# RWKV-7's triangular block inverses: transposed blocks, inversion by columns, scaling after the blocks are gathered

## The chip, the cores and the metric

The kernel runs on one core of a Trainium2 chip. The metric is the device time of one execution in microseconds (us). The kernel before was timed in 3 runs: 1908.01, 1912.06 and 1916.1 us, median 1912.06. One further execution was taken with the hardware profiler; all views quoted below come from it.

A core has five engines that each work through their own instructions in order: TensorE (PE; its weight loads are shown as PEld), VectorE (DVE), ScalarE (ACT), GpSimd (POOL) and SyncE (SP), which here issues DMA transfers. They wait for each other by semaphores.

## The reference

A small model of two layers is run in float32 over a prompt and a sample batch: a gated-delta-net mixer, a ConvFFN, an RWKV-7 mixer, a ConvFFN. The change touches only the RWKV-7 mixer, whose recurrence per head is

```python
def rwkv_step(S, xs):                       # S: [value, key]
    r, d, k, v, kk, a = xs
    sa = einsum('bhvk,bhk->bhv', S, -kk)
    S  = S * d[..., None, :] + sa[..., None] * (kk * a)[..., None, :] \
         + v[..., None] * k[..., None, :]
    return S, einsum('bhvk,bhk->bhv', S, r)
```

where `kk` is a key scaled to unit norm: it is divided by the root of its sum of squares. The kernel does not step through time. It takes chunks of 64 tokens. Inside a chunk the removal terms `sa` of the 64 tokens depend on each other through a strictly triangular 64x64 matrix L of key-by-key products, each row scaled by the inverse of the key's squared norm, and the kernel needs the inverse of I + L for each of 16 heads and each of 9 chunks (chunk 0 has 48 tokens: three blocks of 16).

## The kernel before, in words

The activations stand as 560 columns (prompt and samples) on 128 partitions. Dense layers split every float32 weight tile into a high part (`hi`, line 70, ACT) and a low part (`lo`, line 71, DVE), and multiply with three reduced-precision float32 passes on PE (`dense_g`, line 115, tile `pd`): for every weight tile two columns' halves, four matmuls with `hi` and two with `lo`.

The RWKV mixer lies between about 975 and 1440 us of the profiled span. Its dense work is written as "slots", and the chunk work as "chains", Python generators that a small scheduler (`Weave`, line 359) interleaves: a step says how much PE time it takes and how long its result needs, and a step that isn't due leaves room for the next dense piece. So the order on PE is fixed when the kernel is built; a tile framework then puts the instructions of every engine in an order by a simulated timeline. On the chip each engine simply takes them in that order and waits where an operand isn't ready.

The stages that matter here, for each half G of the heads (G=0 and G=1, 8 heads each):

- `early(G)` (from line 1379): for each of the 9 chunks, eight key-by-key products per chunk on PE (line 1392), masked by DVE out of PSUM into a tile `L` of a ring of two (line 1396), each head's rows scaled by the inverse squared norms `ssq` on ACT (line 1398: 8 instructions for each chunk, 144 in all), and the diagonal blocks sent by DMA to DRAM (`LI0`, line 1373, for chunk 0; `LI`, line 1378). Each chunk has two 32x32 blocks per head.
- `inverse0(G)` gathers the 24 blocks of 16x16, one block on each partition, into the tile X (line 1422), inverts them, and stores them to `UI0` (line 1425). `inverse(G)` does the same with 128 blocks of 32x32 (lines 1406 and 1409). Both halves use the same tile X, so that its loads wait for the stores before. The results are scattered to the matrices A (line 1415, called XX in the trace for one pair of chunks, and line 1430), whose 64x64 form is then made by `merge` (line 1435) for two chunks at a time, four times in a chain: a DVE transposition (line 1439), 16 matmuls (line 1443), an ACT copy (1444), 16 matmuls (line 1448), an ACT copy (line 1449).
- `tri_inplace` (line 1011) is the inversion: GpSimd sets the diagonal to 1 (line 1014); then, row by row from the last one up, a DVE multiplication (line 1023) makes the products for the sums in a tile `tmp` (called `tri` in the trace) and a DVE reduction along the free axis (line 1025) puts the negated sums into X. The multiplication reads X along rows and writes `tmp` transposed (`t.rearrange("p n j -> p j n")`), so that the reduction can run along contiguous elements: the distance between two elements written one after the other is the length of a sum. The tile `tmp` holds 384 elements for each partition, so that a row of 32x32 blocks is done in up to three pieces.
- `rec(G)` (from line 1571) is the recurrence over the chunks. Its DVE steps (lines 1565, 1644, 1652 among them) alternate with PE steps (lines 1624, 1633, 1642, 1651), and it needs the merged blocks. While `rec(0)` does its first chunks, DVE is still inverting the blocks of `inverse(1)`.

Of the kernel before, what the change touches and what calls it, by code (L numbers as in the profile page):

```python
# [8 lines left out]
F32 = mybir.dt.float32  # L9
F32R = mybir.dt.float32r  # L10
I32 = mybir.dt.int32
AF = mybir.ActivationFunctionType
ALU = mybir.AluOpType
AX = mybir.AxisListType
# [3 lines left out]
P = 128  # L18
AHEAD, WB = 1, 2
NRAW = 4  # L20
T = 560
# [988 lines left out]

def tri_inplace(E, X, tmp, n, R):

    nc = E.nc
    nc.gpsimd.memset(X.rearrange("p a b -> p (a b)")[:n, 0:R * R:R + 1], 1.0)  # L1014
    N = tmp.shape[1]
    for i in range(R - 2, -1, -1):
        m = R - 1 - i
        step = min(m, N // m)
        for c1 in range(R, i + 1, -step):
            c0 = max(c1 - step, i + 1)  # L1020
            m1, k = c1 - i - 1, c1 - c0
            t = tmp[:n, :m1 * k].rearrange("p (a b) -> p a b", a=k)
            nc.vector.tensor_tensor(t.rearrange("p n j -> p j n"), X[:n, i + 1:c1, c0:c1],  # L1023
                                    X[:n, i, i + 1:c1].unsqueeze(2).to_broadcast([n, m1, k]), op=ALU.mult)
            nc.vector.tensor_reduce(X[:n, i, c0:c1], t, axis=AX.X, op=ALU.add, negate=True)
        yield


# [22 lines left out]
def rwkv(E, xp, norm, x_dram, sink):  # L1051


    nc, I, O = E.nc, E.I, E.O
    st = ExitStack()
    with st:
        ar = E.pool("rw", 1, stack=st)
        dp = E.pool("rwd", 1, DRAM, stack=st)
        pg = E.pool("pr", 4, PSUM, stack=st)
        bank = bank_of(pg)  # L1060

        KR = ar.tile([P, KD, 9, 2, 64], F32, tag="KR", name="KR")
# [43 lines left out]
        pa = dense(E, [KD], xs, 280)  # L1106
# [48 lines left out]
        for i, r in enumerate((dn, up)):  # L1155
            nc.scalar.activation(th[i][r], la[r], AF.Copy if i == 0 else AF.Tanh)
            if i:
                nc.scalar.activation(la[r], la[r], AF.Tanh)
            nc.vector.tensor_tensor(tl[r], la[r], th[i][r].bitcast(F32), op=ALU.subtract)
            nc.scalar.activation(th[i][(up, dn)[i]], la[r], AF.Copy)  # L1160


        XX, H = big(E, F32, "XX", 0), big(E, F32, "H", 1)
# [129 lines left out]
        def sums(m, sq):  # L1293

            pt = bank([9, 2])
            for c in range(9):
                o, n = col64(c)
                nc.tensor.matmul(pt[64:128, c, :], lhsT=sq[:, o:o + 64], rhs=blk2, start=True, stop=True)
            nc.vector.tensor_copy(ssq[64:128, :, 2 * m:2 * m + 2], pt[64:128])
            if m % 4 == 3:  # L1300
                hs = slice(2 * m - 6, 2 * m + 2)
                q = ssq[64:128, :, hs]
                nc.vector.tensor_scalar(q, q, 1e-6, None, op0=ALU.add)
                nc.vector.reciprocal(q, q)
                nc.vector.tensor_scalar(nw[64:128, :, hs], q, -1.0, None, op0=ALU.mult)
                W.chain(early(m // 4))
            yield 0.6, 0.5, 1


        stA = ExitStack()  # L1310
# [71 lines left out]
        def early(G):  # L1382

            while not decayed >= set(range(4 * G, 4 * G + 4)):
                yield None
            for c in range(9):
                n = col64(c)[1]
                pa = [bank([4, 64]) for hh in range(2)]
                for u in range(4):
                    for hh in range(2):  # L1390
                        r = slice(64 * hh, 64 * hh + 64)
                        nc.tensor.matmul(pa[hh][up, u, :n], lhsT=KB[r, 4 * G + u, c, 1, :], rhs=KR[r, 4 * G + u, c, 1, :n], start=True, stop=True)
                L = E.xp.tile([P, T], F32, tag="s", name="L", bufs=2)[up, :512].rearrange("p (h t) -> p h t", h=8)[:, :, :n]
                mk = mask0[up, 1] if c == 0 else mask[up, 64:128]
                for hh in range(2):
                    nc.vector.tensor_tensor(L[:, hh::2], pa[hh][up, :, :n], mk.unsqueeze(1).to_broadcast([64, 4, n]), op=ALU.mult)
                for h in range(8):
                    nc.scalar.activation(L[:, h], L[:, h], AF.Copy, scale=ssq[up, c, 8 * G + h:8 * G + h + 1])
                to_inverse(G, c, L)
                yield 0.9, E.d2, 2  # L1400

# [2 lines left out]
        def inverse(G):  # L1404
            X, tmp = B["X"], B["tmp"]
            nc.sync.dma_start(out=X, in_=LI[G].rearrange("j c h i t -> (j c h) i t"))
            for _ in tri_inplace(E, X, tmp, P, 32):
                yield 0, E.d3, 0
            nc.sync.dma_start(out=UI[G].rearrange("j c h i t -> (j c h) i t"), in_=X)
# [10 lines left out]
        def inverse0(G):  # L1420
            X = B["X"].rearrange("p a b -> p (a b)")[:24, :256].rearrange("p (a b) -> p a b", a=16)
            nc.sync.dma_start(out=X, in_=LI0[G].rearrange("j h i t -> (j h) i t"))
            for _ in tri_inplace(E, X, B["tmp"], 24, 16):
                pass
            nc.sync.dma_start(out=UI0[G].rearrange("j h i t -> (j h) i t"), in_=X)
# [437 lines left out]
def prep(a):  # L1863
# [56 lines left out]
    def rput(name, m):  # L1920
        rc[:, RC[name]:RC[name] + m.shape[1]] = m
    rput("mask", np.concatenate([i64[:, None] <= a64[None], i64[:, None] < a64[None]], 1) * 1.0)
    b64 = np.where(i64 < 48, np.minimum(i64 // 4, 8), 9)
    same = b64[:, None] == blk[None]
    rput("mask0", np.concatenate([same & (i64[:, None] <= a48[None]), same & (i64[:, None] < a48[None])], 1) * 1.0)
    b = (ar[:, None] // 64 == ar[None] // 64) * 1.0
    rput("blk", b)
# [112 lines left out]
```

## Time and profile before

| | before |
|---|---|
| median of 3 runs | 1912.06 us |
| the profiled execution | 1913.3 us |
| its span on the core | 1911.3 us |
| mean granted TensorE clock | 0.95 |
| PE busy | 1801.1 us (94%) |
| DVE busy | 1154.5 us (60%) |
| ACT busy | 803.9 us (42%) |
| GpSimd busy | 369.0 us (19%) |

A line `L1023` names line 1023 of the kernel before. A group such as `tri<-X` names the tile written and the tile read. `x124` is a count. In a view by windows each engine has its busy time in a stretch of the span and its instructions; `PEclk` is the clock that TensorE was granted, 1.00 being full speed. In a timeline the brackets at the end of a row hold the idle time of that engine just before it and what ended it. In the chain that ended last, each row is a piece of work or a transfer on which the end of the program depended.

The four inversions lie at 1008.4 to 1040 us (`inverse0(0)`), 1047.1 to 1131.4 us (`inverse(0)`), 1138.7 to 1156.5 us (`inverse0(1)`) and 1162.8 to 1231.5 us (`inverse(1)`).

### The profile page before, as it was taken

The numbers are of one execution on the slowest core, as the hardware profiler recorded it, in microseconds if no ns is written. First come the engines' busy times: TensorE is split into PE (matmuls) and PEld (weight loads), VectorE is DVE, ScalarE is ACT, GpSimd is POOL, SyncE is SP. The second block draws the span as 40 slices with busy tenths as digits, with TensorE's granted clock in tenths as the row PEclk, the third lists the DMA queues.
The fourth block names the chain that finished last, engine by engine and source line by source line (L and its number), as shares of the span: only waits on it lengthen the run. The fifth ranks groups of instructions, "written<-read, shape, count | busy, mean of one in ns | idle before, by whom it ended". The sixth has DMA issues, their size and how long they took to land.

```text
span 1911.3 us, 36670 instructions
## 1 busy us (share of the span) xinstructions
PE 1801.1 (94%) x14673; PEld 1718.5 (90%) x14673; DVE 1154.5 (60%) x2221; ACT 803.9 (42%) x1779; POOL 369.0 (19%) x616
## 2 busy tenths in 40 slices
PE   7999999999999999998989999799997999999996
PEld 6889998789999999998778997788786999999996
DVE  6698973875555553337787977874555555554223
ACT  4766434442222222222976535554644322222221
POOL 3442403621222220013110000021001111111011
PEclk9999998999999999999898999896898999999998
DMA  4233232433222223444122244332235322223331
GB/s 131 76 91 93 70 90 104 150 122 120 82 89 89 80 87 104 120 155 98 48 70 62 70 117 121 98 91 80 78 102 163 123 89 89 89 88 91 99 109 67
DMA packets 128010, 186.13 MB, mean 97 GB/s; under 512 B 63088, under 2 KB 75376, under 8 KB 127840
## 3 DMA queue, kind: packets, MB, share of 16 engines
q10 hardware_dynamic: 34448, 111.63, 18.7%
q1 hardware_dynamic: 93392, 72.17, 13.0%
q8 instruction: 116, 1.90, 0.4%
q14 instruction: 54, 0.44, 0.1%
HBM read 151.56 MB, written 32.18 MB: 96 GB/s over the span
## 4 chain that ended last, share of the span: by engine, by line
PE 76%; DVE 12%; ACT 3%; DMA 3%; issue 1%; POOL 0%; SPq 0%; DVEq 0%; ACTq 0%
PE pd L115 56%; PE pd L138 3%; PE pg L1353 1%; DVE lo L71 1%; PE pg L1739 1%; PE pg L1628 1%; DVE it L425 1%; PE pg L1624 1%; PE pg L1651 1%; PE pg L1642 1%; DVE tri L1023 1%; PE pg L835 1%; PE pg L1633 1%; DVE cv L593 1%; DMA xd<-xo 1%
## 5 line engine op out<-in xcount | busy, mean ns | idle before, releaser
L115 PE MATMUL pd<-x,hi 128*128 128x280 f32 (+7 forms) x4768 | 837.5, 297 | 23.5 <-ACT hi L70 9.1
L115 PEld LDWEIGHTS pd<-x,hi 128*128 128x128 f32 (+1 forms) x4768 | 695.4, 192 | 30.8 <-ACT hi L70 9.3
L115 PE MATMUL pd<-x,lo 128*128 128x296 f32 (+5 forms) x2384 | 516.4, 297 | 5.6 <-DVE lo L71 5.6
L70 ACT ACTIVATE hi<-raw 128x1024 fp32r<-128x1024 f32 (+3 forms) x218 | 219.8, 1009 | 481.7 <-PE pd L115 447.4
L115 PEld LDWEIGHTS pd<-x,lo 128*128 128x128 f32 (+1 forms) x2384 | 382.9, 192 | 9.9 <-DVE lo L71 6.8
L71 DVE TENSOR_TENSOR lo<-raw,hi 128x1024 fp32r<-128x1024 f32 (+3 forms) x218 | 255.7, 1173 | 219.1 <-ACT hi L70 212.6
L218 POOL TENSOR_TENSOR s<-s,sq 128x560 f32<-128x560 f32 (+2 forms) x30 | 50.8, 1693 | 303.7 <-ACT sq L216 273.9
L304 DVE TENSOR_TENSOR gp<-pd,s 128x528 f32<-128x528 f32 (+1 forms) x44 | 30.8, 701 | 105.9 <-PE pd L115 105.9
L115 PE MATMUL pd<-hl,hi 128*128 128x280 f32 (+1 forms) x448 | 93.5, 290 | 0.0
L115 PE MATMUL pd<-hh,hi 128*128 128x280 f32 (+1 forms) x448 | 93.3, 290 | 0.0
L115 PE MATMUL pd<-hh,lo 128*128 128x280 f32 (+1 forms) x448 | 93.3, 290 | 0.0
L316 ACT ACTIVATE gs<-cv 128x528 f32<-128x528 f32 (+1 forms) x44 | 28.1, 639 | 147.3 <-DVE cv L314 147.3
L115 PE MATMUL pd<-hb,hi 128*128 128x280 f32 (+1 forms) x512 | 85.8, 290 | 0.0
L115 PEld LDWEIGHTS pd<-hb,hi 128*128 128x128 f32 x512 | 72.8, 188 | 0.0
L115 PEld LDWEIGHTS pd<-hh,lo 128*128 128x128 f32 x448 | 70.8, 188 | 0.0
L115 PEld LDWEIGHTS pd<-hh,hi 128*128 128x128 f32 x448 | 70.6, 188 | 0.0
L115 PEld LDWEIGHTS pd<-hl,hi 128*128 128x128 f32 x448 | 70.5, 188 | 0.0
L319 POOL TENSOR_TENSOR gs<-gs,s 128x560 f32<-128x560 f32 (+1 forms) x44 | 60.8, 1382 | 38.1 <-ACT gs L317 38.1
L322 DVE TENSOR_TENSOR h<-pd,gs 128x560 f32<-128x560 f32 (+1 forms) x44 | 32.1, 730 | 57.0 <-POOL gs L319 57.0
L308 POOL COPY fnew<-gp 128x2 f32<-128x2 f32 x44 | 8.1, 185 | 291.5 <-DVE gp L304 291.5
L1023 DVE TENSOR_TENSOR tri<-X 128x4 f32<-128x4 f32 (+26 forms) x124 | 56.0, 451 | 5.2 <-POOL X L1014 2.2
L138 PE MATMUL pd<-os,hi 128*128 128x280 f32 x256 | 52.8, 303 | 2.5 <-ACT os L183 1.9
(539 smaller groups left out, 3039.6 us busy)
## 6 DMA issues: line engine op xcount, KB each, us to landing
raw<-w_up ACTq DMA_DIRECT2D x88, 512.0 KB, 3.3
raw<-w_in ACTq DMA_DIRECT2D x32, 512.0 KB, 3.3
raw<-w_down ACTq DMA_DIRECT2D x32, 512.0 KB, 3.6
raw<-w_down ACTq DMA_DIRECT2D x16, 384.0 KB, 3.0
kbd<-kst SPq DMA_DIRECT2D x18, 256.0 KB, 2.0
KB<-kbd SPq DMA_DIRECT2D x18, 256.0 KB, 3.0
xd<-xo SPq DMA_DIRECT2D x16, 280.0 KB, 2.1
raw<-gdn_out ACTq DMA_DIRECT2D x8, 512.0 KB, 3.3
```

Of the source, the lines that this page charges most:

```text
L70: nc.scalar.activation(hi[:R, :kt, :M], raw[:R, :kt, :M], AF.Copy)
L71: lo_eng.tensor_tensor(lo[:R, :kt, :M], raw[:R, :kt, :M], hi[:R, :kt, :M].bitcast(F32), op=ALU.subtract)
L115: nc.tensor.matmul(ps[b][:M, :c1 - c0] if isinstance(ps, list) else ps[:M, b, :c1 - c0], lhsT=w[:, kk, :M], rhs=x[:, c0:c1], start=(k == 0 ...
L138: nc.tensor.matmul(ps[:, b, :c1 - c0], lhsT=a, rhs=x[:, c0:c1], start=(k == i == 0), stop=(k == len(xs) - 1 and i == 2))
L218: nc.gpsimd.tensor_tensor(self.acc[:, :self.w], self.acc[:, :self.w], sq, op=ALU.add)
L304: nc.vector.tensor_tensor(two(gp[:, m0:]), pm, two(s[:, mo:mo + ml]), op=ALU.mult)
L316: nc.scalar.activation(gs[:, mo:mo + ml], cv[:, m0 - 2:], AF.Silu)
L319: nc.gpsimd.tensor_tensor(gs, gs, s[:, :n_main], op=ALU.mult)
L322: nc.vector.tensor_tensor(two(h), ps[:, :, :hw], two(gs), op=ALU.mult)
L425: nc.vector.tensor_tensor(t.rearrange("p n j -> p j n"), U[:n, i:R, c0:], L[:n, i, i:R].unsqueeze(2).to_broadcast([n, m, k]), op=ALU.mult)
L593: nc.vector.scalar_tensor_tensor(cv, gp[:, i:i + 584], cw[i], cv, op0=ALU.mult, op1=ALU.add)
L1023: nc.vector.tensor_tensor(t.rearrange("p n j -> p j n"), X[:n, i + 1:c1, c0:c1], X[:n, i, i + 1:c1].unsqueeze(2).to_broadcast([n, m1, k]), ...
```

## The change

Five things are done differently.

1. In `early`, the two operands of the key-by-key matmuls change places, so that the blocks come out transposed (and on partitions 0 to 63). The mask is a transposed constant `maskT`, loaded once. The 144 ACT scalings are gone.
2. The inverse squared norms are brought into the order of the blocks: `by_block`, once for each half, copies `ssq` on ACT, transposes it on PE (72x64), copies it on ACT and stores it to DRAM (`Dd`).
3. `inverse` and `inverse0` load them with two and three small DMAs for each half, and one DVE multiplication for each scales all of X (128x1024 and 24x256).
4. `tri_inplace` goes by columns from the first to the last: the products are now written as they are read, contiguously, and the reduction puts a column of sums into X, whose elements lie one row of X apart.
5. As the sums of a column take the place of the upper half, a DVE memset sets the row's lower half to zero after each column.

By the sizes in the code, the 32x32 inverse has 43 multiplications and 43 reductions over 8671 elements for each partition in place of 47 and 47 over 8450, and 31 memsets; the 16x16 inverse has 15 and 15 over 1240 elements as before, and 15 memsets. Over the four inversions that is 116 multiplications in place of 124, 116 reductions in place of 124, 19822 elements in place of 19380, and 92 memsets.

```diff
 def tri_inplace(E, X, tmp, n, R):
     nc.gpsimd.memset(X.rearrange("p a b -> p (a b)")[:n, 0:R * R:R + 1], 1.0)
     N = tmp.shape[1]
-    for i in range(R - 2, -1, -1):
-        m = R - 1 - i
-        step = min(m, N // m)
-        for c1 in range(R, i + 1, -step):
-            c0 = max(c1 - step, i + 1)
-            m1, k = c1 - i - 1, c1 - c0
-            t = tmp[:n, :m1 * k].rearrange("p (a b) -> p a b", a=k)
-            nc.vector.tensor_tensor(t.rearrange("p n j -> p j n"), X[:n, i + 1:c1, c0:c1],
-                                    X[:n, i, i + 1:c1].unsqueeze(2).to_broadcast([n, m1, k]), op=ALU.mult)
-            nc.vector.tensor_reduce(X[:n, i, c0:c1], t, axis=AX.X, op=ALU.add, negate=True)
+    for j in range(1, R):
+        i = 0
+        while i < j:
+            w = j - i
+            k = min(w, N // w)
+            t = tmp[:n, :k * w].rearrange("p (a b) -> p a b", a=k)
+            nc.vector.tensor_tensor(t, X[:n, i:i + k, i:j], X[:n, j, i:j].unsqueeze(1).to_broadcast([n, k, w]), op=ALU.mult)
+            nc.vector.tensor_reduce(X[:n, i:i + k, j], t, axis=AX.X, op=ALU.add, negate=True)
+            i += k
+        nc.vector.memset(X[:n, j, 0:j], 0.0)
         yield
...
+        maskT = nw[dn].rearrange("p a b -> p (a b)")[:, :112]
+        nc.sync.dma_start(out=maskT, in_=I["maskT"])
...
+                by_block(m // 4, q)
                 W.chain(early(m // 4))
...
+        D, D0 = E.rest[:, 0:32], E.rest[:24, 32:48]
+        def by_block(G, q):
+            pt = bank([64])
+            s = E.xp.tile([P, T], F32, tag="s", name="Dt", bufs=2)
+            t = s[:72, :64]
+            nc.scalar.activation(s[up, 64:136].rearrange("p (c h) -> p c h", c=9), q, AF.Copy)
+            nc.tensor.transpose(pt[:72], s[up, 64:136], E.ident[up, up])
+            nc.scalar.activation(t, pt[:72], AF.Copy)
+            nc.sync.dma_start(out=Dd[G], in_=t)
...
-                        nc.tensor.matmul(pa[hh][up, u, :n], lhsT=KB[r, 4 * G + u, c, 1, :], rhs=KR[r, 4 * G + u, c, 1, :n], start=True, stop=True)
+                        nc.tensor.matmul(pa[hh][dn, u, :n], lhsT=KR[r, 4 * G + u, c, 1, :], rhs=KB[r, 4 * G + u, c, 1, :n], start=True, stop=True)
...
-                    nc.vector.tensor_tensor(L[:, hh::2], pa[hh][up, :, :n], mk.unsqueeze(1).to_broadcast([64, 4, n]), op=ALU.mult)
-                for h in range(8):
-                    nc.scalar.activation(L[:, h], L[:, h], AF.Copy, scale=ssq[up, c, 8 * G + h:8 * G + h + 1])
+                    nc.vector.tensor_tensor(L[:, hh::2], pa[hh][dn, :, :n], mk.unsqueeze(1).to_broadcast([64, 4, n]), op=ALU.mult)
...
             nc.sync.dma_start(out=X, in_=LI[G].rearrange("j c h i t -> (j c h) i t"))
+            for j in range(2):
+                nc.sync.dma_start(out=D[64 * j:64 * j + 64], in_=Dd[G, 8:72, 32 * j:32 * j + 32])
+            nc.vector.tensor_tensor(X, X, D.unsqueeze(1).to_broadcast([P, 32, 32]), op=ALU.mult)
...
             nc.sync.dma_start(out=X, in_=LI0[G].rearrange("j h i t -> (j h) i t"))
+            for j in range(3):
+                nc.sync.dma_start(out=D0[8 * j:8 * j + 8], in_=Dd[G, :8, 16 * j:16 * j + 16])
+            nc.vector.tensor_tensor(X, X, D0.unsqueeze(1).to_broadcast([24, 16, 16]), op=ALU.mult)
```

The order of the instructions moves with it. Line numbers of the changed kernel are 23 higher at the merge and in `rec` (its line 1462 is line 1439 before, 1466 is 1443, 1492 is 1469, 1537 is 1514), and the reduction of `tri_inplace` is its line 1024.

On VectorE, at the end of `inverse(0)`, the rows of the kernel before run from the last piece of that inverse to the first transposition of `merge` (XX is the matrix A of the first chunks, TY the transposed blocks):

```order
1187 L1023 TENSOR_TENSOR tri<-X 128x19x12
...
1189 L1023 TENSOR_TENSOR tri<-X 128x7x7
1190 L71 TENSOR_TENSOR lo<-raw,hi 128x1024
1191 L1025 TENSOR_REDUCE X<-tri 128x7
1192 L71 TENSOR_TENSOR lo<-raw,hi 128x1024
1193 L1023 TENSOR_TENSOR tri<-X 24x1
1194 L1025 TENSOR_REDUCE X<-tri 24x1
1195 L1023 TENSOR_TENSOR tri<-X 24x2x2
1196 L1025 TENSOR_REDUCE X<-tri 24x2
1197 L1023 TENSOR_TENSOR tri<-X 24x3x3
1198 L1025 TENSOR_REDUCE X<-tri 24x3
1199 L1439 STREAM_TRANSPOSE TY<-XX 32x512
```

The same place in the changed kernel (line 1026 is the memset, line 1445 the scaling of the 24 blocks by the norms in the tile `rest`, lines 1528 to 1537 are steps of `products` and of the samples that stood before the inverse's end until now):

```order
1222 L1023 TENSOR_TENSOR tri<-X 128x361
1223 L1379 TENSOR_TENSOR A<-pg,rc 128x4x128
1224 L1024 TENSOR_REDUCE X<-tri 128x19
1225 L1026 MEMSET X 128x31
1226 L71 TENSOR_TENSOR lo<-raw,hi 128x1024
1227 L1379 TENSOR_TENSOR A<-pg,rc 128x4x128
1228 L1537 TENSOR_TENSOR H<-pg,H 128x280
1229 L1528 TENSOR_TENSOR prod<-KR,KB 128x48
1230 L1537 TENSOR_TENSOR H<-pg,H 128x280
1231 L1529 TENSOR_TENSOR prod<-KR,KB 128x512
...
1233 L1445 TENSOR_TENSOR X<-X,rest 24x256
1234 L1462 STREAM_TRANSPOSE TY<-XX 32x512
```

The first transposition now stands ahead of the whole of `inverse0(1)`, behind its scaling; six other steps stand between the inverse's end and it.

On TensorE, the first matmul of `merge` in the kernel before (its neighbours are the dense matmuls of the v layer, which also fill the 44 rows ahead of the first one shown):

```order
4845 L115 MATMUL pd<-x,hi 128x280 x4
4846 L115 MATMUL pd<-x,lo 128x280 x2
4847 L115 MATMUL pd<-x,hi 128x280 x4
4848 L115 MATMUL pd<-x,lo 128x280 x2
4849 L115 MATMUL pd<-x,hi 128x280
4850 L1443 MATMUL pg<-TY,XX 32x32 x16
4851 L1469 MATMUL pg<-cm,ks 128x128 x4
4852 L1513 MATMUL pg<-prod,brk 128x280 x2
```

The same place in the changed kernel:

```order
4792 L1515 MATMUL pg<-cm,H 64x128
4793 L115 MATMUL pd<-x,hi 128x280 x4
4794 L115 MATMUL pd<-x,lo 128x280 x2
4795 L115 MATMUL pd<-x,hi 128x280 x4
4796 L115 MATMUL pd<-x,lo 128x280 x2
4797 L115 MATMUL pd<-x,hi 128x280 x4
4798 L115 MATMUL pd<-x,lo 128x280 x2
4799 L115 MATMUL pd<-x,hi 128x280 x4
4800 L115 MATMUL pd<-x,lo 128x280 x2
4801 L115 MATMUL pd<-x,hi 128x280 x4
4802 L1466 MATMUL pg<-TY,XX 32x32 x16
4803 L1492 MATMUL pg<-cm,ks 128x128 x4
```

Counted over the whole program, 1285 `hi` and 642 `lo` dense matmuls of the form 128x280 stand ahead of the first merge matmul before, and 1220 and 608 now: it has moved up by 99 dense matmuls. Ahead of the first matmul of `rec` (line 1594 before) stand 1344 and 672 before, 1322 and 660 now: 34 dense matmuls that were ahead of the recurrence now stand among its first chunks.

On VectorE, at the fourth transposition of `merge` in the kernel before, which stands just ahead of the first columns of `inverse(1)`:

```order
1235 L1506 TENSOR_TENSOR prod<-KR,KB 128x512
1236 L1508 TENSOR_SCALAR brk<-rc,pv 128x128
1237 L71 TENSOR_TENSOR lo<-raw,hi 128x1024
1238 L1439 STREAM_TRANSPOSE TY<-A 32x512
1239 L1023 TENSOR_TENSOR tri<-X 128x1
1240 L1025 TENSOR_REDUCE X<-tri 128x1
```

and in the changed kernel:

```order
1292 L1529 TENSOR_TENSOR prod<-KR,KB 128x512
1293 L1531 TENSOR_SCALAR brk<-rc,pv 128x128
1294 L1426 TENSOR_TENSOR X<-X,rest 128x1024
1295 L1462 STREAM_TRANSPOSE TY<-A 32x512
1296 L1023 TENSOR_TENSOR tri<-X 128x1
1297 L1024 TENSOR_REDUCE X<-tri 128x1
1298 L1026 MEMSET X 128x1
```

The scaling of the 128 blocks of `inverse(1)` has come to stand between, and with it the wait for their load into X.

More of the change, by code (lines that the diff above doesn't have):

```diff
@@ L1305, in sums @@
                 nc.vector.tensor_scalar(nw[64:128, :, hs], q, -1.0, None, op0=ALU.mult)
+                by_block(m // 4, q)
                 W.chain(early(m // 4))
             yield 0.6, 0.5, 1
+        Dd = dp.tile([2, 72, 64], F32, tag="Dd", name="Dd")
+        D, D0 = E.rest[:, 0:32], E.rest[:24, 32:48]
[7 more added lines that the diff above has]
+            nc.sync.dma_start(out=Dd[G], in_=t)
         stA = ExitStack()
@@ L1391, in early @@
                         r = slice(64 * hh, 64 * hh + 64)
-                        nc.tensor.matmul(pa[hh][up, u, :n], lhsT=KB[r, 4 * G + u, c, 1, :], rhs=KR[r, 4 * G + u, c, 1, :n], start=True, stop=True)
-                L = E.xp.tile([P, T], F32, tag="s", name="L", bufs=2)[up, :512].rearrange("p (h t) -> p h t", h=8)[:, :, :n]
-                mk = mask0[up, 1] if c == 0 else mask[up, 64:128]
+                        nc.tensor.matmul(pa[hh][dn, u, :n], lhsT=KR[r, 4 * G + u, c, 1, :], rhs=KB[r, 4 * G + u, c, 1, :n], start=True, stop=True)
+                L = E.xp.tile([P, T], F32, tag="s", name="L", bufs=2)[dn, :512].rearrange("p (h t) -> p h t", h=8)[:, :, :n]
+                mk = maskT[:, 64:] if c == 0 else maskT[:, :64]
                 for hh in range(2):
-                    nc.vector.tensor_tensor(L[:, hh::2], pa[hh][up, :, :n], mk.unsqueeze(1).to_broadcast([64, 4, n]), op=ALU.mult)
-                for h in range(8):
-                    nc.scalar.activation(L[:, h], L[:, h], AF.Copy, scale=ssq[up, c, 8 * G + h:8 * G + h + 1])
+                    nc.vector.tensor_tensor(L[:, hh::2], pa[hh][dn, :, :n], mk.unsqueeze(1).to_broadcast([64, 4, n]), op=ALU.mult)
                 to_inverse(G, c, L)
@@ L1924, in prep @@
     same = b64[:, None] == blk[None]
+    d["maskT"] = np.concatenate([a64[:, None] > a64[None], (same & (i64[:, None] > a48[None]))[:64]], 1).astype(f)
     rput("mask0", np.concatenate([same & (i64[:, None] <= a48[None]), same & (i64[:, None] < a48[None])], 1) * 1.0)
```

## The prediction

> **What bounds the kernel now.** I read the page first, then the windows of the RWKV mixer, the waits and the chain there, and last the timeline at the first merge.
>
> ```profile
> span 1911.3 us, 36670 instructions
> PE 1801.1 (94%) x14673; PEld 1718.5 (90%) x14673; DVE 1154.5 (60%) x2221; ACT 803.9 (42%) x1779; POOL 369.0 (19%) x616
> ```
>
> TensorE is the bound: 110 us of the span at most are to be had without taking work from it, and the change takes none. So a gain can only come out of PE's gaps in the mixer. The windows show where these are; the columns are the stretch, its length, busy time and instructions of PE, PEld, DVE, ACT and POOL, the granted clock, DMA share, GB/s.
>
> ```profile
> 995.00:1012.00 17.00, 9.03 (x104) 8.24 (x102) 16.09 (x32) 14.22 (x42) 5.01 (x7) 0.59 0.19 45
> 1012.00:1140.00 128.00, 128.00 (x1094) 120.38 (x1095) 105.78 (x242) 61.94 (x174) 7.29 (x11) 0.98 0.31 88
> 1047.00:1131.40 84.40, 84.40 (x703) 79.18 (x702) 77.48 (x165) 41.60 (x108) 7.01 (x9) 1.00 0.31 89
> 1140.00:1175.00 35.00, 33.71 (x409) 30.61 (x407) 22.83 (x69) 17.83 (x36) 1.29 (x3) 0.90 0.46 120
> 1175.00:1232.00 57.00, 42.66 (x363) 35.53 (x364) 53.25 (x135) 32.86 (x99) 4.25 (x6) 0.86 0.32 91
> 1232.00:1300.00 68.00, 62.04 (x596) 54.05 (x595) 46.84 (x116) 38.89 (x122) 12.10 (x29) 0.96 0.39 100
> ```
>
> From 1012 to 1140 us PE is busy throughout, so nothing that DVE or ACT saves there shortens anything by itself. Two gaps remain: 995 to 1012 (8.0 us idle, DVE 16.09 of 17 busy) and 1175 to 1232 (14.3 us idle, DVE 53.25 of 57), the first chunks of the recurrence, with `inverse(1)` between its steps on DVE. The chain in the second gap and PE's waits from 1140 to 1240 say the same:
>
> ```profile
> 1181.31 0.60 DVE tri L1023
> 1182.39 0.68 DVE tri L1023
> ...
> 1226.85 0.80 DVE tri L1023
> 1227.69 0.54 DVE X L1025
> ```
> ```profile
> PE pg L1642 <- DVE KB L1565: 5.4, 3, 3.1
> PE pg L1685 <- ACT KB L1681: 3.8, 2, 2.3
> PE pg L1443 <- DVE TY L1439: 1.3, 1, 1.3
> ```
>
> **The inversion by columns.** First its instructions, over the stretches of `inverse(0)`, `inverse(1)` and the second gap; the multiplications (line 1023), then the reductions (line 1025):
>
> ```profile
> 1047.00:1133.00 86.00, 23.94 (x47) 1.00 0.31 88
> 1158.00:1233.00 75.00, 23.21 (x47) 0.87 0.35 101
> 1175.00:1232.00 57.00, 20.14 (x35) 0.86 0.32 91
> ```
> ```profile
> 1047.00:1133.00 86.00, 15.84 (x47) 1.00 0.31 88
> 1175.00:1232.00 57.00, 13.75 (x36) 0.86 0.32 91
> ```
>
> and what single instructions of the two forms take:
>
> ```profile
> 1094.20 0.20 DVE L1505 TENSOR_TENSOR prod<-KR,KB 128x48 f32<-128x48 f32 x1
> 1094.31 0.68 DVE L1506 TENSOR_TENSOR prod<-KR,KB 128x512 f32<-128x512 f32 x1
> ...
> 1099.58 1.09 DVE L1023 TENSOR_TENSOR tri<-X 128x384 f32<-128x384 f32 x1
> 1101.70 0.54 DVE L1025 TENSOR_REDUCE X<-tri 128x16 f32<-128x384 f32 x1
> ...
> 1102.85 0.85 DVE L1023 TENSOR_TENSOR tri<-X 128x375 f32<-128x375 f32 x1
> ```
>
> A contiguous multiplication costs 0.15 us and 1.04 ns for each element (0.48 us over the 464 elements between 48 and 512). The transposed write of 384 elements takes 1.09 us, twice the 0.55 us that this line gives; of 375 elements 0.85 for 0.54. The reduction of 384, which reads contiguously, is on the line. So a 32x32 inverse by columns costs 43 x 0.15 + 8671 x 1.04 ns = 15.5 us in multiplications in place of 23.94 (−8.4), and 43 reductions over nearly as many elements 15.5 in place of 15.84 (−0.4).
>
> [...]
>
> What is added on DVE: the scaling of X, 1024 elements, on the same line 1.22 us, and 256 elements 0.42. And 31 memsets for each 32x32 inverse, of 1 to 31 elements, plus 30 for the small ones. No DVE memset is in the trace. The nearest rows are the smallest multiplication and GpSimd's memset:
>
> ```profile
> 1163.23 0.16 DVE L1023 TENSOR_TENSOR tri<-X 128x4 f32<-128x4 f32 x1
> 1163.43 0.16 DVE L1025 TENSOR_REDUCE X<-tri 128x2 f32<-128x4 f32 x1
> L1014 POOL MEMSET X<- x4: 114/138/165, 1006.5 to 1162.6; 24x16 f32 x2, 128x32 f32 x2
> ```
>
> From one to the next of these DVE rows are 0.20 us (1163.23 to 1163.43), so a memset costs at most about 0.20; a memset depends on the reads of the row ahead of it but nothing waits for it soon, so that it could overlap down to 0.05. I take 0.10, between them, as it has no operand to read: 3.1 us for an inverse, 1.6 to 6.2. The sum for one 32x32 inverse is −8.4 −0.4 +1.2 +3.1 = −4.5 us of DVE time (−6.0 to −1.4). The small inverses have no gain to speak of (1240 elements) and gain 15 memsets each, +1.9 us.
>
> **The early blocks.** 144 ACT instructions go:
>
> ```profile
> L1398 ACT ACTIVATE L<-L,ssq x144: 313/328/346, 1000.0 to 1068.3; 64x64 f32<-64x64 f32 x128, 64x48 f32<-64x48 f32 x16
> DVE L L1396 <- DMA LI<-L: 6.2, 4, 2.6
> ```
>
> At 0.33 us each that is 2.6 us of latency for a chunk, from the mask to the DMA that frees the ring of two `L` tiles. In the stretch where PE is full it lies beside PE (ACT 61.94 of 128 us busy): 0. Ahead of 1012 the chain that ended last goes through it once:
>
> ```profile
> 1000.03 1.95 ACT L L1398 x8
> 1002.90 1.51 DMA LI<-L
> 1004.53 0.77 DVE L L1396 x2
> ```
>
> There 1.95 us go, but DVE has only 0.9 us idle in 995 to 1012 and is next on that path; `by_block` adds two small ACT copies and a ring slot. I take −1.0 (−2 to 0). The swap of operands, the transposed mask and the small DMAs on SP I put at 0: the matmuls keep count and size, and SP's loads of `D` for G=1 wait for the scaling of G=0, with 14 block stores queued behind them, whose cover is PE's full stretch to 1140.
>
> **The first merge.** In the changed order it stands 99 dense matmuls earlier and the recurrence 34. This is its chain in the kernel before, and the dense rate:
>
> ```profile
> 1130.07 0.68 PE L115 MATMUL pd<-x,hi 128*128 128x280 f32 x4
> 1130.09 1.23 DVE L71 TENSOR_TENSOR lo<-raw,hi 128x1024 fp32r<-128x1024 f32 x1 [0.25 <-ACT hi L70]
> ...
> 1130.85 0.68 PE L115 MATMUL pd<-x,hi 128*128 128x280 f32 x4
> ...
> 1131.49 0.33 SPq L1409 DMA_DIRECT2D UI<-X  x1
> ...
> 1137.30 4.65 SPq L1415 DMA_DIRECT2D XX<-UI  x8
> ...
> 1142.36 0.70 DVE L1439 STREAM_TRANSPOSE TY<-XX 32x512 f32<-32x512 f32 x1 [2.58 <-DMA XX<-UI]
> ...
> 1143.20 1.17 PE L1443 MATMUL pg<-TY,XX 32*32 32x32 f32 x32 [1.26 <-DVE TY L1439]
> ```
>
> Six dense matmuls take 0.78 us (1130.07 to 1130.85), so 99 are 12.8 us and 34 are 4.4. PE came to the merge at 1143.2 − 1.26 = 1141.9; now it comes at 1141.9 − 12.8 − 1.0 = 1128.1. From the inverse's end (1131.4) to the first merge matmul were 11.8 us, nearly all DMA, which stay. `inverse(0)` ended at 1131.4 with 77.48 of 84.4 us of DVE busy, so its DVE work shortens it: −4.5 by itself, and about −3.8 for what the new order sets behind it (a dense split, 1.23, the `prod` steps, 0.68 and 0.20, two `H` steps of 280 elements, 0.44 each by the contiguous line, and some small ones), and about −2 for an earlier start, since the blocks of G=0 come without the scalings. That ends it at 1121, the merge is ready at 1133, and PE waits 4.7 us where it waited 1.26: +3.4 (+2 to +6, the latter with half a clock after a wait; the clock was 0.59 in the gap at 995). The fourth transposition now has the scaling of X ahead of it, with its wait for the load: +1 (0 to +2).
>
> **The second gap.** The multiplications there fall from 20.14 to about 13.0 us (×15.5/23.94), −7.1, the reductions by 0.3; memsets for some 24 columns add 2.4. DVE gets about 5.0 us less to do where it is 93% busy, and PE follows it, not one to one, as some steps wait for ACT or PE: −4.0 (−7 to −1). The 34 dense matmuls fill gaps that PE has there while it waits for line 1565: −4.4 (−4.4 to −2), as they were on PE's full stretch before.
>
> The sum: −1.0 + 3.4 + 1.0 − 4.0 − 4.4 = −5.0, and the 6.0 us that PE idles from 1232 to 1300 give −1, my choice, as `inverse(1)` leaves DVE sooner: −6.0. Against the profiled execution, 1913.3, that is 1907.3. The median of the runs is 1912.06, so I forecast 1906. About 0.5% (9.6 us) is what a measurement of this kernel can tell from no change.
>
> **Rivals.** (a) *The second gap nearly closes.* For it: DVE is 93% busy there, and the chain runs through lines 1023 and 1025. `inverse(1)` now begins earlier, and the merges too. Then −7 and −4.4 there, and −2 early, against +2 at the merge, and −2 of the idle time behind 1232: −13.4 with the +1 of the fourth transposition left out, so 1898.6 on the median. Against it: PE also waits there for ACT (3.8 us for line 1681). Chance 0.30.
>
> (b) *The merge comes too early for its blocks: slower.* The planned order has the merge 12.8 us earlier, but PE gets there on its own. If `inverse(0)` on the chip ends only about 3 us sooner (memsets at 0.20, no earlier start because the gather of X waits for SP's queue, and DVE waits for dense splits inside it), the merge is ready at 1140 and PE stands 12 us there, +10.7; 2 us at half clock behind it, 2 at the fourth transposition, −4.4 and −1 in the second gap make +9.3, 1921.4 on the median. It decides the sign when the inverse ends after about 1127, since each later us costs one. Against it: 8.4 us of DVE are firm. Chance 0.12.
>
> (c) *Memsets eat the gain.* At 0.20 us each, the upper bound, a 32x32 inverse keeps −1.4 us, and a 16x16 one gains 15 x 0.20 + 0.42 = 3.4, so that over the four nothing is saved. The second gap gives −1 at most, `inverse(0)` ends 3 us later and the merge takes +6: with −4.4, −1 and +1, it is 1912.7. Chance 0.13. [...]
>
> (d) That the transposed write isn't the cause of the price would leave the multiplications at 23.94 us: the rows of one size in one inverse make this 0.03, with a time as in (b).
>
> The forecast as such has the rest, 0.42, its own range 1902 to 1910. **Chances:** faster by over 0.5% (below 1902.5) is most of (a) and the low end of the forecast, 0.33; slower (above 1921.6) about half of (b) and (d), 0.08; the rest 0.59. The range leaves out about a tenth at each side: 1896 to 1920.
>
> **What would show it.** Line 1023's multiplications at 0.55 us for 384 elements and about 38 us in all; a memset at 0.05 to 0.20; PE waiting for line 1462 3 to 6 us at the first merge; PE idle below 8 us in the stretch of the first recurrence chunks. PE waiting 10 us or more at the merge means (b); DVE's busy time of the inversions unchanged means (c). The forecast is wrong if the second gap keeps its 14 us.

## The result and the profile after

The changed kernel takes 1900.1 us on the median of 20 runs (1889.66 to 1913.5), the kernel before 1912.09 us beside it (1902.75 to 1924.47, 20 runs). The ratio is 0.9938, with a 95% interval of 0.9919 to 0.9958: 12 us faster, where 6 were forecast and 1896 to 1920 was the range. The profiled execution has a span of 1892.0 us, 19 us less than that of before, at the short end of its runs.

```profile
span 1892.0 us, 36613 instructions
PE 1782.0 (94%) x14675; PEld 1702.7 (90%) x14675; DVE 1144.7 (61%) x2301; ACT 768.8 (41%) x1639; POOL 366.8 (19%) x616
```

TensorE was busy for 1801.1 us before and for 1782.0 now, though it has the same work but for two small transpositions. Its idle time is the same (110.2 and 110.0 us; 107.2 and 105.9 in a second profile of each). So what went is busy time: the same matmuls ran faster (in the stretch E below, 1130 of them were busy for 125.1 us before and 109.2 us now). That was in no term of my sum, and most of this document is about it.

First the terms that were there. The groups of the inversion by columns, with the least, median and greatest duration in ns:

```profile
L1023 DVE TENSOR_TENSOR tri<-X x116: 138/299/598, 1007.4 to 1216.1; 128x1 f32<-128x1 f32 x4, 128x9 f32<-128x9 f32 x4, 128x25 f32<-128x25 f32 x4, 128x49 f32<-128x49 f32 x4
...
L1026 DVE MEMSET X<- x92: 59/68/84, 1011.1 to 1217.2; 24x1 f32 x2, 24x2 f32 x2, 24x3 f32 x2, 24x4 f32 x2
```

The multiplications and the memsets over the whole stage, busy us in the third column:

```profile
900.00:1300.00 400.00, 38.66 (x116) 0.93 0.32 89
```
```profile
900.00:1300.00 400.00, 6.40 (x92) 0.93 0.32 89
```

So the multiplications cost 38.7 us in place of 56.0 (38 was forecast), a memset 0.07 us in place of 0.10. The windows of the stage, to be laid beside those of before:

```profile
995.00:1012.00 17.00, 10.54 (x107) 10.04 (x108) 16.36 (x37) 5.67 (x10) 3.72 (x7) 0.55 0.22 49
1012.00:1140.00 128.00, 127.74 (x1175) 120.07 (x1175) 106.76 (x324) 41.22 (x79) 6.64 (x12) 0.98 0.34 95
1140.00:1175.00 35.00, 33.59 (x385) 30.73 (x384) 23.81 (x81) 18.69 (x41) 2.34 (x3) 1.00 0.46 132
1175.00:1232.00 57.00, 45.02 (x381) 38.88 (x383) 41.70 (x123) 31.05 (x97) 3.44 (x8) 0.82 0.31 92
```

VectorE is no longer the bound from 1175 to 1232 us: 41.70 us busy where it was 53.25, though in part because the recurrence now begins 12 us earlier in this window. Yet TensorE still idles 12.0 us there (14.3 before), at a clock of 0.82 (0.86). The stretch from 1140 to 1175 us runs at full clock, where it had 0.90. The first merge, in the timeline (SPq is a DMA issue):

```profile
1114.77 0.53 SPq L1429 DMA_DIRECT2D UI<-X  x1
...
1118.94 5.17 SPq L1435 DMA_DIRECT2D XX<-UI  x8
...
1122.30 0.70 DVE L1462 STREAM_TRANSPOSE TY<-XX 32x512 f32<-32x512 f32 x1 [0.39 <-DMA XX<-UI]
...
1125.21 1.19 PE L1466 MATMUL pg<-TY,XX 32*32 32x32 f32 x32
```

`inverse(0)` ended at 1114.7 us, not at 1121. The transposed blocks were there at 1123.0, and TensorE came at 1125.2 and did not wait at all.

To see where the time went I took the first and last starts of four groups, which stand at the same dense work in both kernels: the first products (line 1353), the first recurrence chunk (1624), the first gate matmul (1547) and the last recurrence matmul (1651). Before:

```profile
L1353 PE MATMUL pg<-KR,KB x288: 271/272/374, 1080.6 to 1277.7; 64*128 64x128 f32 x144
...
L1624 PE MATMUL pg<-KB,KR x128: 274/276/582, 1187.3 to 1401.0; 128*128 128x128 f32 x128
...
L1547 PE MATMUL pg<-gs,hi x32: 288/295/603, 1280.2 to 1294.9; 128*128 128x280 f32 x32
...
L1651 PE MATMUL pg<-KB,A x192: 218/222/369, 1243.1 to 1414.6; 128*64 128x64 f32 x168, 64*64 64x64 f32 x24
```

After:

```profile
L1372 PE MATMUL pg<-KR,KB x288: 272/272/373, 1078.0 to 1267.9; 64*128 64x128 f32 x144
...
L1647 PE MATMUL pg<-KB,KR x128: 275/275/580, 1175.2 to 1376.9; 128*128 128x128 f32 x128
...
L1570 PE MATMUL pg<-gs,hi x32: 287/293/398, 1270.4 to 1283.9; 128*128 128x280 f32 x32
...
L1674 PE MATMUL pg<-KB,A x192: 218/222/369, 1234.0 to 1390.4; 128*64 128x64 f32 x168, 64*64 64x64 f32 x24
```

That gives three stretches: **Q**, products and merges up to the recurrence, 106.7 us before and 97.2 after; **R**, the first half's recurrence, 92.9 and 95.2; **E**, gates, merges and recurrence of the second half, 134.4 and 120.0. The greatest part of the difference of the two profiles, 14.4 us, lies in E, which the change does not touch. Ahead of Q 2.6 us are saved, and behind E, where the work is the same too, 4.9 are lost (496.7 and 501.6 us up to the end); with Q and R that makes the 19. The clock shows the part in E, before and then after (10 us rows, the clock is the column behind the engines):

```profile
1300.00:1310.00 10.00, 10.00 (x152) 9.07 (x148) 4.50 (x7) 2.43 (x5) 2.74 (x6) 0.76 0.45 134
1310.00:1320.00 10.00, 10.00 (x77) 9.02 (x76) 1.83 (x4) 3.59 (x13) 1.19 (x5) 0.50 0.16 37
1320.00:1330.00 10.00, 10.00 (x75) 7.61 (x74) 2.21 (x5) 6.08 (x18) 0.66 (x1) 0.50 0.12 36
1330.00:1340.00 10.00, 10.00 (x89) 9.03 (x88) 4.50 (x17) 6.10 (x22) 0.39 (x1) 0.54 0.34 101
```
```profile
1290.00:1300.00 10.00, 9.96 (x136) 9.08 (x134) 3.77 (x7) 3.69 (x10) 2.82 (x6) 0.83 0.40 119
1300.00:1310.00 10.00, 9.27 (x128) 7.45 (x126) 3.36 (x7) 7.23 (x23) 0.92 (x5) 1.00 0.27 72
1310.00:1320.00 10.00, 9.85 (x99) 8.90 (x99) 4.90 (x17) 5.22 (x17) 0.79 (x1) 0.66 0.33 101
1320.00:1330.00 10.00, 10.00 (x116) 8.47 (x117) 3.77 (x7) 4.76 (x15) 1.04 (x1) 1.00 0.26 85
```

Before, TensorE is busy without a pause for some 30 us and has half the clock all the while. After, no row of 10 us in E is at half the clock (the lowest, from 1310 us, is 0.66), and the row from 1320 us on is at 1.00.

### The profile page after: what moved, and what is told of

It is laid out like the page before. It is cut to its first block, busy times and chain, and to the rows that moved or that the text cites. A ratio compares the mean times of both kernels' runs of the same rounds, so it can differ in the third digit from the quotient of the medians.

```text
span 1892.0 us, 36613 instructions
## 1 busy us (share of the span) xinstructions
PE 1782.0 (94%) x14675; PEld 1702.7 (90%) x14675; DVE 1144.7 (61%) x2301; ACT 768.8 (41%) x1639; POOL 366.8 (19%) x616
## 4 chain that ended last, share of the span: by engine, by line
PE 77%; DVE 9%; ACT 4%; DMA 3%; issue 1%; SPq 0%; DVEq 0%; ACTq 0%
PE pd L115 58%; PE pd L138 3%; PE pg L1372 1%; PE pg L1674 1%; PE pg L1651 1%; DVE lo L71 1%; PE pg L1647 1%; PE pg L1665 1%; PE pg L1656 1%; PE pg L835 1%; PE pg L627 1%; DMA xo<-x 1%; PE pg L1762 1%; DMA xs<-xd 1%; PE pg L1466 1%
## 5 line engine op out<-in xcount | busy, mean ns | idle before, releaser
L304 DVE TENSOR_TENSOR gp<-pd,s 128x528 f32<-128x528 f32 (+1 forms) x44 | 30.8, 701 | 106.8 <-PE pd L115 106.7
L115 PE MATMUL pd<-hb,lo 128*128 128x280 f32 (+1 forms) x256 | 53.3, 289 | 0.0
```

The costliest lines, as they stand in the source:

```text
L115: nc.tensor.matmul(ps[b][:M, :c1 - c0] if isinstance(ps, list) else ps[:M, b, :c1 - c0], lhsT=w[:, kk, :M], rhs=x[:, c0:c1], start=(k == 0 ...
L304: nc.vector.tensor_tensor(two(gp[:, m0:]), pm, two(s[:, mo:mo + ml]), op=ALU.mult)
```

## The experiments

Two theories stood against each other. **T**: the gain is VectorE's, whose inversion got shorter. **O**: the gain is the order's, with blocks that come earlier and merges that stand earlier; VectorE's saving is hidden beside a busy TensorE. A third question came with the profile: whether the low clock in E belongs to the kernel before or to chance. Ratios are to the kernel before, timed beside each.

**The two kernels profiled again.**

> The kernel before once more, for a second profile. If the 31 us at half the clock that the first profile shows from 1302 to 1333 us belong to the kernel, they come again there; if they are chance of one execution, that stretch takes 20 to 23 us.

> The changed kernel once more, for a second profile: the way from the first key product to the first recurrence chunk again 12 us shorter than before if that is the change's doing; within 5 us of before if it was chance.

Before once more: Q 104.5, R 94.2, E 134.4 us, a time of 1917.47 us. After once more: Q 97.2, R 95.1, E 119.9 us, 1894.44 us. The first expectation's first half came true: the stretch at half the clock is there again, at the same work (by rows of 5 us from 1310 to about 1339 us in the first profile, not from 1302 to 1333, and from 1315 to 1345 in the second). Counted from the first key product (line 1392), the way to the first recurrence chunk is 15.2 us shorter in the first pair of profiles and 13.0 in the second, as the second expectation had it; but 40 dense matmuls, some 5 us, stand ahead of that product now instead of behind it. Q, which holds the same work in both kernels, is 8.4 us shorter on the mean of two.

**Contiguous writes alone, in the order of before.**

> The kernel before with one thing changed: the products are written contiguously into tri, so that the sums that follow are over other elements. Same instructions in the same order on every engine, the scalings stay, no memsets. Theory T (the change gains because VectorE's inversion gets shorter): line 1023 falls from 56.0 to about 38 us, inverse(0) ends 8 us earlier but its merge keeps its late place, so only the 1.26 us of PE's wait there and the gap of the recurrence can gain: -4 to -8 us. Rival O (the change gains because the blocks come earlier and the merges stand earlier, VectorE's saving being hidden beside PE): line 1023 falls all the same, the time stays within 2 us of before.

> The kernel before with contiguous writes, as timed already (-10 us on the median, 0.9948 of before), to make its interval narrow enough to be told from the changed kernel's. T: it keeps more than half of the changed kernel's gain, -7 to -10 us. O: it was chance, -4 us or less.

```diff
-            nc.vector.tensor_tensor(t.rearrange("p n j -> p j n"), X[:n, i + 1:c1, c0:c1],
+            nc.vector.tensor_tensor(t.rearrange("p a b -> p (a b)").rearrange("p (n j) -> p n j", n=m1), X[:n, i + 1:c1, c0:c1],
```

Ratio 0.9948 (0.9922 to 0.9975), and 0.9957 (0.9935 to 0.9979) the second time: medians 9.6 and 8.3 us below before's. The price of the transposed write is settled. Of one form, busy us and mean ns, before and then here:

```profile
L1023 DVE TENSOR_TENSOR tri<-X 128x378 f32<-128x378 f32 x4 | 3.6, 907 | 0.1
```
```profile
L1023 DVE TENSOR_TENSOR tri<-X 128x378 f32<-128x378 f32 x4 | 2.2, 550 | 0.1
```

But `inverse(0)` does not end sooner. This is its end in the second profile:

```profile
1129.13 0.21 DVE L1023 TENSOR_TENSOR tri<-X 128x49 f32<-128x49 f32 x1
1130.52 1.23 DVE L71 TENSOR_TENSOR lo<-raw,hi 128x1024 fp32r<-128x1024 f32 x1 [1.18 <-ACT hi L70]
1131.66 0.20 DVE L1025 TENSOR_REDUCE X<-tri 128x7 f32<-128x49 f32 x1
```

The last reduction stands behind a dense split, and the split waits for ScalarE's high part. That is the last of several such waits, and the smaller part. VectorE's waits for TensorE between the steps of the inverse grew from 2.2 to 9.6 us (1040 to 1135 us). These are the longest waits, those for ScalarE among them (us in all, how many, the longest):

```profile
DVE L L1396 <- PE pd L115: 2.8, 1, 2.8
DVE lo L71 <- ACT hi L70: 2.5, 2, 1.4
DVE XX L1360 <- PE pg L1353: 2.3, 3, 1.0
DVE KR L1205 <- PE pd L115: 2.2, 3, 1.2
```

VectorE had 72.10 us of work from 1047 us to that end in place of 77.48, and ended at 1131.9 us in place of 1131.4: waits took the place of the work saved. R is 2 to 4 us shorter (90.4 and 90.8), as T has it for the gap. E is 124.2 and 127.5 us.

**Strided writes in the order of the changed kernel.**

> The changed kernel with one thing put back: the products are written with the distance of a column's length between neighbours, so that the sums are over other elements. Same instructions in the same order as the changed kernel. T: line 1023 rises from about 38 to 55 us, inverse(0) ends about 8 us later, PE waits about 6 us at the first merge and VectorE has 7 us more in the gap of the recurrence: most of the gain goes, -3 to +3 us against before. O: the blocks come early enough anyway, -8 to -12 us as in the changed kernel.

> The changed kernel with strided writes, as timed already (-8 us on the median, 0.9938 of before), for the same reason. T: -3 us or less. O: -8 to -12 us. A third reading is open after the first look: each half is enough by itself, and both stay near -9.

```diff
-            nc.vector.tensor_tensor(t, X[:n, i:i + k, i:j], X[:n, j, i:j].unsqueeze(1).to_broadcast([n, k, w]), op=ALU.mult)
+            nc.vector.tensor_tensor(tmp[:n, :k * w].rearrange("p (b a) -> p a b", a=k), X[:n, i:i + k, i:j], X[:n, j, i:j].unsqueeze(1).to_broadcast([n, k, w]), op=ALU.mult)
```

Ratio 0.9938 (0.9902 to 0.9973) and 0.9941 (0.9916 to 0.9966): the changed kernel's own, 0.9938. O and the third reading hold, T falls for the total: once the order is the new one, the 15 us that the strided write adds (line 1023 at 53.71 us) cost nothing that these runs can tell. The merge shows why, in the second profile:

```profile
1117.35 0.32 SPq L1429 DMA_DIRECT2D UI<-X  x1
...
1124.44 0.70 DVE L1462 STREAM_TRANSPOSE TY<-XX 32x512 f32<-32x512 f32 x1 [0.38 <-DMA XX<-UI]
...
1127.20 1.19 PE L1466 MATMUL pg<-TY,XX 32*32 32x32 f32 x32
```

Even with slow multiplications the inverse ends at 1117.3 us, and TensorE doesn't wait. Q is 97.6 and 99.1 us, R 97.0 and 97.2: two us more than in the changed kernel in R, where VectorE's saving is used. Contiguous writes alone gain 8 to 10 us and the new order with strided writes 8 to 12, which together would be more than the 12 of the whole change: these two do not add up.

**The parts of the change, one at a time, in the kernel before.**

> The kernel before without the 144 ScalarE scalings of the blocks (left out; the mask step multiplies by 0.001 as well); the inversion stays by rows with transposed writes. Its first merge stands 27 dense matmuls earlier than before. T: inverse(0) begins some us earlier, PE's wait at the merge stays or grows, -2 to +2 us. O: the blocks without the scalings are half of the gain or more, -5 to -8 us.

```diff
-                    nc.vector.tensor_tensor(L[:, hh::2], pa[hh][up, :, :n], mk.unsqueeze(1).to_broadcast([64, 4, n]), op=ALU.mult)
-                for h in range(8):
-                    nc.scalar.activation(L[:, h], L[:, h], AF.Copy, scale=ssq[up, c, 8 * G + h:8 * G + h + 1])
+                    nc.vector.scalar_tensor_tensor(L[:, hh::2], pa[hh][up, :, :n], 1e-3, mk.unsqueeze(1).to_broadcast([64, 4, n]), op0=ALU.mult, op1=ALU.mult)
```

Ratio 0.9958 (0.9928 to 0.9988), median −4.5 us: between the two expectations, nearer to O (by the ratio −8). Q 101.3, R 98.3, E 121.3 us.

> The kernel before with the inversion of the changed kernel alone (by columns, contiguous, with memsets; the blocks are not transposed, so that what is inverted is another matrix); the scalings stay, no scaling of X. Its first merge stands 30 dense matmuls earlier than before. T: most of the gain, -6 to -10 us. O: less than a third of it, 0 to -4 us. A memset is expected at 0.06 us, as the changed kernel shows.

```diff
-    for i in range(R - 2, -1, -1):
...
+    for j in range(1, R):
+        i = 0
+        while i < j:
...
+        nc.vector.memset(X[:n, j, 0:j], 0.0)
         yield
```

Ratio 0.9962 (0.9934 to 0.999), median −8.6 us: as T had it. Q 101.6, R 97.5, E 119.1 us. The two parts together (4.5 and 8.6 us) are about the 12 of the whole change; with intervals of some 6 us to each side, these two runs can't tell whether they add up.

**The parts of the change put back or left out, in the changed kernel.**

> The changed kernel with 144 ScalarE instructions put back between the mask and the transfers of the blocks; they multiply by one. Its first merge stands 2 dense matmuls later than in the changed kernel. If the scalings on the way of the blocks are worth the 4 us that leaving them out of the kernel before gave, -6 to -8 us against before are left. If the shorter inversion alone carries the gain, -10 to -12 us.

```diff
+                for h in range(8):
+                    nc.scalar.activation(L[:, h], L[:, h], AF.Copy, scale=1.0)
                 to_inverse(G, c, L)
```

Ratio 0.9927 (0.99 to 0.9954): the scalings cost the changed kernel nothing. This run tells more by its profile, of an execution at the long end of its runs (1909.82 us, where the median is 1900.75). Its Q is 98.1 us, but its E is 133.4, and there the clock is low:

```profile
1294.00:1304.00 10.00, 10.00 (x93) 8.90 (x91) 2.78 (x4) 2.05 (x4) 1.53 (x5) 0.52 0.41 125
1304.00:1314.00 10.00, 10.00 (x98) 9.08 (x97) 1.97 (x4) 3.99 (x13) 2.23 (x5) 0.50 0.13 34
1314.00:1324.00 10.00, 10.00 (x78) 8.19 (x77) 1.68 (x4) 5.71 (x16) 0.00 (x0) 0.50 0.15 39
```

TensorE's groups of matmuls have one and the same order there in this kernel, in the changed kernel and in the kernel before, so the changed order can fall into the same hole. That this is what spreads the changed kernel's own times is read from their clocks (0.945 at 1913.5 us, 0.963 at 1889.66), not from a profile of a long one. R is 92.3 us in this profile, 3 less than in the two of the changed kernel.

> The changed kernel without the 92 memsets (left out; the sums then take in the lower halves). The order on TensorE stays that of the changed kernel. Memsets are 0.06 to 0.08 us in its profile, some 3 us for one 32x32 inverse. T: PE does not wait for the first merge now, so only the gap of the recurrence gains, 0 to -3 us against the changed kernel, -11 to -15 against before. Rival (the memsets eat half of the gain): -17 us or more against before.

```diff
-        nc.vector.memset(X[:n, j, 0:j], 0.0)
```

Ratio 0.9936 (0.9905 to 0.9967), 12 us: the rival falls. Without the memsets R is 91.8 us, 3 less, but the time can't be told from the changed kernel's.

**The low clock by itself.** In the stretch E the merges of the second half issue 32x32 matmuls. Four idle matmuls were put between the two steps of each merge, in both kernels:

```diff
             nc.scalar.activation(TY[r2], py[r2], AF.Copy)
             yield 1.0, 1.0, 1
+            if G == 1:
+                pz = bank([4, P])
+                for h in range(4):
+                    nc.tensor.matmul(pz[:, h], lhsT=E.ident, rhs=E.ident, start=True, stop=True)
+                yield 1.0, 0.5, 1
```

> The kernel before with 16 idle matmuls more (identity by identity, 128x128, four in one step of each of the four merges of G=1; nothing reads them), 4.4 us of TensorE work at full clock in the stretch where both profiles of before show about 30 us at half the clock behind 1305 us. If the clock stays low there because the small matmuls of the merges don't keep it up, the stretch from the first gate matmul to the last recurrence matmul falls from 134 to 125 us or less, and the time by 5 us or more. If the low clock there doesn't depend on what TensorE does, the time rises by 4 us.

> The changed kernel with the same 16 idle matmuls. Its two profiles have that stretch at 120 us, but its times lie in two heaps, 1890 to 1899 and 1901 to 1913 us. If the fillers hold the clock up, the median falls to 1897 us or less and the upper heap goes; if not, it rises by 4 us, to -8 against before.

The kernel before gets faster by doing more: ratio 0.9963 (0.9942 to 0.9984), median 1905.55 us, −6.0, for 4.4 us of added TensorE work. Its E is 123.2 us in the one profile taken, where both profiles without the fillers have 134.4; R (92.3) is as before, and Q (103.4), which ends ahead of the fillers, near it. None of its 12 runs has a mean clock below 0.952; of the 30 of the kernel before beside them 18 have. The clock in the same stretch:

```profile
1300.00:1310.00 10.00, 10.00 (x148) 8.98 (x148) 4.13 (x6) 2.29 (x5) 3.83 (x10) 1.00 0.53 139
1310.00:1320.00 10.00, 8.19 (x108) 7.35 (x107) 2.82 (x9) 9.40 (x34) 0.00 (x0) 0.89 0.27 71
1320.00:1330.00 10.00, 10.00 (x89) 9.10 (x89) 5.32 (x17) 4.54 (x16) 0.00 (x0) 0.60 0.14 42
1330.00:1340.00 10.00, 10.00 (x127) 8.14 (x126) 4.46 (x8) 3.67 (x11) 2.09 (x2) 1.00 0.38 118
```

This shows that the low clock can be kept away with all the former work still there, but not that it is the idle matmuls themselves that do it. Their step in the chain also moves other work: the merge matmuls that stood ahead of a long group of other matmuls (line 1443 at 1305.9 us, line 1739 at 1310.1) now stand behind it (1308.2 and 1305.6). And the one stretch at half clock that is left, 1319 to 1328 us, ends before the third group of idle matmuls starts at 1329.7. A kernel with the step and without its matmuls was not run.

The changed kernel with the fillers has a median of 1899.95 us (ratio 0.9931, 0.9905 to 0.9956): no faster, where 1897 or less was expected, but its 7 runs lie between 1894.85 and 1902.71 us, where the 20 of the changed kernel reach 1913.5. The upper part of the heap is gone, as the fillers' reading had it, though 7 runs are few: a third of the changed kernel's lie above 1903. The added work may take back what that gives. It isn't a version to keep instead. But the two filled kernels, timed side by side, give the change's gain with the long stretch out of both: 1905.55 against 1899.95 us, 5.6 us in place of 12, with few runs (6.2 on the mean, roughly 3 to 10).

## Why the prediction was right, and where it was not

The range and the sign held; the size was half, and the sum got near in good part by luck. Its frame was that "a gain can only come out of PE's gaps", and its −6.0 us are all idle time of TensorE. That idle time fell by 0.7 us on the mean of two profiles each (108.7 to 108.0), and the gain came out of busy time. Of the signs I had set, the multiplications and the memset came true; TensorE's 3 to 6 us of waiting at the first merge (none) and an idle time below 8 us in the second gap (12.0) did not.

**Prices.** Multiplications (38.7 us for 38 forecast), the scalings of X (1.23 and 0.41) and the memsets (0.07 for 0.10, chosen between 0.20 from the rows and 0.05, a guess that no row gave) were right or near; the 0.20 us of rival (c) was too high. The transposed write is what made the old form slow: contiguous writes alone took 907 ns for 378 elements down to 550.

**The first merge: the step that failed.** I let the inverse's end follow from VectorE's work ("its DVE work shortens it") and got a wait of 4.7 us, +3.4. In the old order less work changed its end by half a us, since steps of other work in VectorE's queue wait there for TensorE and ScalarE (9.6 and 2.5 us in the second profile with contiguous writes); in the new order, with a split and the `prod` steps behind it, it ended at 1114.7 us, and at 1117.3 even with strided writes. The start was also earlier than I took it: the first column came at 1041.8 us where it had been 1047.1, and I had allowed 2. The wait went from 1.26 us to nothing, −1.3 where +3.4 was forecast. Half a clock after a wait, in the upper end of that term and in rival (b), was an estimate from the 0.59 in the gap at 995; with no wait at the merge it was not put to the test. The fourth transposition, put at +1.0, kept TensorE waiting in neither kernel. Rival (b), which needed a late inverse, was far off.

**The second gap: right cause, wrong fate.** VectorE's busy time fell by 11.6 us from 1175 to 1232 us, more than I had (its inverse also ends sooner, at 1217 us, and the recurrence began sooner); over R it fell by 5.3 (73.4 to 68.1 us), near the 5.0 forecast. But R did not get shorter: 93.6 us on the mean of two before, 95.2 after. With the same order the saving is 2 us (95.2 against 97.1 with strided writes), 3 in the old order (90.6 for 93.6); the new order with strided writes has 3 to 4 us more than the kernel before, but the run with the scalings put back, in nearly the new order, has 92.3, so that a cost of the order isn't firm. My −4.0 is −2. Less waiting for VectorE did not close the gap: TensorE idles for 12.3 and 10.9 us in R, where it was 12.5 and 11.4. Much of its time there is its own matmuls at a low clock (0.67 and 0.50 in the two rows from 1185 to 1205 us); whether that is what holds R up was not tried.

The −4.4 for the 34 moved dense matmuls was a misplaced overlap: none of them gets into the second gap. In the changed kernel the last dense matmuls run ahead of the first recurrence chunk, where TensorE is busy:

```profile
1170.57 0.43 PE L115 MATMUL pd<-x,lo 128*128 128x280 f32 x2
...
1175.18 1.16 PE L1647 MATMUL pg<-KB,KR 128*128 128x128 f32 x8 [1.43 <-DVE KB L1635]
```

What was gained ahead of the recurrence lies in Q, which holds the same dense work in both kernels: 105.6 us on the mean of two before, 97.2 now. In the first profiles 2.6 us of that are idle time (4.1 to 1.6); the rest is busy time, at a clock that was 0.90 from 1140 to 1175 us and is 1.00 now. Not all of Q is the clock: in the kernel before with the fillers the clock over Q is 1.00 (so in each row of 10 us from 1130 to 1180 us), and Q is still 103.4 us, 6 more than in the changed kernel, 4 of them idle (5.6 for 1.6).

**The small terms.** The early blocks were put at −1.0: TensorE's idle time from 995 to 1012 us went from 8.0 to 6.5 us. The −1 from 1232 to 1300 us was −0.4 (6.0 to 5.6 us of idle time).

**The term that was missing** is the clock. Over 221 timed executions of these ten kernels a straight line for each kernel, with one slope for all, gives 1.39 us for each 0.001 of mean granted clock. The mean clock is 0.9503 for the kernel before (88 runs) and 0.9553 for the changed one (21): 7 us of its 13 on the mean. At equal clock it is 5.8 us faster. That is near the 5.6 us between the filled kernels, and near my −6.0 by number alone, since mine was to come out of the gaps. The parts of the change do the same in smaller: 0.9547 for contiguous writes and for strided writes in the new order. The fillers raise the kernel before to 0.9562 while at equal clock they leave it at +0.8 us. This is a line through times and clocks, not an experiment. It would explain why each half seemed enough by itself, if each makes the long stretch at half clock rarer and that gain can be had only once.

What is shown: E is 134.4 us in both profiles of before, 133.4 in that of the changed kernel with scalings put back, and 119 to 128 us in nine others without fillers; and with a step of idle matmuls in E the kernel before is 6 us faster on the median and its low clocks are gone, with an E of 123.2 us in one profile. What stays open: whether the idle matmuls or the changed order of the step does that, and why the clock recovers in one execution and not in another at the same instructions. That each variant's lower time comes from fewer such executions is read from times and mean clocks, not seen in a profile of each run.

Among the rivals, the measured time lies nearest to (a), 1898.6 us, but that is luck, not its mechanism: the second gap did not close.

## What to carry to other kernels

Where an engine works through one queue in order, look at what stands in the queue between a chain's steps before you turn saved work into an earlier end: here 5.4 us less work of VectorE moved the inverse's end from 1131.4 to 1131.9 us, because instructions of other work waited longer between its steps (9.6 us for TensorE in place of 2.2). Look where moved work lands before you let it fill a gap. Count the granted clock as a resource of its own: E, with its one long stretch at half clock, took 134.4 us and without it 120.0, a difference larger than any wait in the sum, and the stretch came and went in code that the change does not touch. And when parts of a change gain as much alone as together, look for one thing that each of them relieves.

## What the hardware showed that I had not expected

- TensorE stayed at about half its clock for nearly 30 us in which it never paused by the profile (1310 to 1340 us before, 0.50 to 0.54), among matmuls of 32x32 to 128x128 and two of 128x512 (the 128x128 ones took 0.44 us there and 0.27 at full clock).
- A step of 16 idle 128x128 matmuls made a kernel 6 us faster (1911.59 to 1905.55 us), by the matmuls or by the order that came with them.
- A VectorE memset of 1 to 31 elements takes 59 to 84 ns, about half of the smallest multiplication (138 ns).
